# Decays, B and C of an SSD branch in scratch tables: another layout, another engine for the stores, an earlier place for sums and loads

## The chip, the cores and the metric

The kernel runs on one core of one Trainium2 chip, in one launch. The metric is device time in microseconds. Three runs of the kernel before took 1981.85, 1986.65 and 1986.39 us; their median is 1986.39 us. The profile is of one execution of its own.

## The reference

The reference is one inference step of a hybrid decoder layer in fp32, for a prompt of 256 tokens and, with the same weights, for 8 sample rows of one token each. With all widths written out:

```
h = RMSNorm(x)                                        # x: 256 + 8 rows of 2048
q, k, v, z, xbc, dt, qm, g = split(h @ w_in)          # w_in: 2048 x 13856
A = sliding-window attention(q, k, v)                 # 16 heads of 64, window 128
B = SSD(xbc, z, dt)                                   # 32 heads of 64 in 4 groups, state 128
M = attention of qm into 256 memory tokens            # 4 heads of 256
x = x + (sig(g0)*(A @ w_up_swa) + sig(g1)*(B @ w_up_ssd) + sig(g2)*(M @ w_up_mem)) @ w_out
x = x + (silu(h2 @ w_gate) * (h2 @ w_up)) @ w_down    # h2 = RMSNorm(x), width 5632
```

The part that the change touches is B, the SSD branch (a Mamba-2 scan in chunks). For the prompt there are two chunks of 128 tokens:

```
xbc = silu(causal conv of 4 taps(xbc));  x, B, C = split(xbc)      # B, C: 4 groups of 128
dt  = softplus(dt + dt_bias);  a = -exp(a_log)
acs = cumsum(dt * a) within the chunk                              # per token and head
decay[l, s] = exp(acs[l] - acs[s]) for s <= l, else 0
y   = sum over s of (C_l . B_s) * decay[l, s] * dt_s * x_s  +  (what the chunk before left) * exp(acs[l])  +  d_skip * x
```

For each of the 8 sample rows the scan is one step: the state (32 heads x 64 x 128) is multiplied by `exp(dt * a)`, `dt * x * B` is added, the new state is an output, and `y = state . C + d_skip * x`. Then y is multiplied by silu(z) and normed by group. The updated states, caches and conv buffers are outputs too.

## The kernel before

**Main stream.** All large products run on TensorE as a list of *units*. A unit is a weight tile of 512 KB (`raw`, 128 x 1024 fp32), loaded by SyncE (L230), split by ScalarE into a rounded part `hi` (L167) and by VectorE into the rest `lo` (L168), and used in 24 matmuls: eight pieces of the tile, each as hi x h_hi, hi x h_lo and lo x h_hi, so that the product keeps fp32 accuracy. Tokens are the moving side, 264 columns (256 prompt and 8 sample rows). `feed(i)` runs ahead of unit `i`: `N_DMA = 4` units in load, `N_SPLIT = 3` in the split, with four buffers for `raw` and three each for `hi` and `lo`.

**Order of the units.** Memory keys and values; then the groups of w_in for the memory queries, window queries, keys and values, the memory gates, B, C, dt; then, for the SSD groups g = 0 to 3, x and z (`x_group`, `z_group`), with the gates and the up-projection of the attention branch between them; the memory up-projection (`pum`); the SSD gates; the SSD up-projection (`pus`); the output projection; and, in three blocks, the feed-forward layers. In the profile's names `pin` is any group of w_in, `pua` the attention's up-projection.

**Side work.** Everything else is written as generators that yield an estimate of their time in us. After each unit the list `side` gets a credit of 1.0 and the list `slow` one of 0.75, at most 3.0 in hand, and the first task of each list runs while credit is left. In `side` stand, per SSD group, the conv (`V`, `ssd_conv_work`), the chunks (`X`, `ssd_chunk_work`) and the norm (`N`); ahead of them `task_b`, `task_c` and `task_dt`. In `slow` stand the memory attention of the sample rows and then, per group, their one-step scan (`Y`, `ssd_sample_work`), which may start when the group's chunks are written. Before the first unit of `pus` both lists are drained.

**The planner.** The kernel is traced in this order, but then a planner orders the instructions of each engine by a simulated time line (`schedule_with_timeline_sim=True`), hands out the tiles' buffers and places the semaphores. An engine takes its instructions in that order, and a DMA is issued by the engine that it is written for: when its wait is not over, all behind it on that engine waits too. Place in the source is thus a priority, not a time: in the profile the load of `bb` for group 0, written behind that group's chunks, goes out at 498 us, before them.

**Around the change.** `task_dt` turns dt to tokens x heads, takes the softplus (L1033 to L1045), and makes `da = dt * a` (L1062). Then come the sample rows' step sizes and factors (`dsc`, L1067 to L1083). Then the sums: `acs` by a matmul with a triangle of ones, once as tokens x heads (`acs_tok`) and once as heads x tokens, which ScalarE copies to `acsT` (L1093) and GpSimd stores to the DRAM scratch `acs_d` (L1094); with `wf` the weights of the chunk states are made. `task_c` puts B and C of the sample rows into the DRAM scratch `bc_d` (L1027). Both tables are there to be read back with one row broadcast to all 128 partitions:

- in `ssd_chunk_work`, per group and chunk, `dec` (L1156): 8 heads x 128 tokens of `acs_d`, 512 KB in SBUF. ScalarE turns it into the decay (L1165, L1166) and, for the second chunk, into `ce` (L1160); VectorE multiplies it by C . B (L1168); TensorE uses it (`py`);
- in `ssd_sample_work`, per group, `bb` and `cbs` (L1217, L1218): B and C of the 8 sample rows, 512 KB each. For each pair of heads there is a state tile `ld` (512 KB, loaded at L559 and stored at L1230); ScalarE scales it (L1225), VectorE adds `dx * bb` (L1226) and sums against `cbs` (L1227).

`dec`, `ce`, the conv's `acc` and `xs`, `y`, and the merge's `mgi` share four buffers (tag `t4`); `bb` and `cbs` share two (tag `lm`) with the tiles of the memory cache; `ld` has two of its own.

Before, `acs_d` is laid out as heads x 256 tokens, so that a `dec` load reads, for each partition, 8 runs of 512 bytes at a distance of 1 KB. `bc_d` is laid out as sample row x (B or C) x group x 128, so that `bb` reads 8 runs of 512 bytes at a distance of 4 KB.

Of the kernel before, what the change touches and what calls it, by code (L numbers as in the profile page):

```python
# [72 lines left out]
def tile_hybrid_decoder_step(  # L73
# [58 lines left out]
    def tiny(name, n):  # L132
        assert n <= 64
        return tp.tile([P, 64], F32, tag="tiny", name=nm(name), bufs=9)[:, 0:n]
# [826 lines left out]
    last = const([P, 11, 24], "last")  # L961
    acs_tok = const([P, 64], "acs_tok")
    wf = const([P, 96], "wf")
    acs_d = dr.tile([32, 256], F32, name="acs_d")
    bc_d = dr.tile([NS, 2, 4, P], F32, name="bc_d")

    def conv(ct, raw, dst):

# [47 lines left out]
    def task_c():  # L1016
        ssd["C"] = const([P, 4, NT], "CT")
        yield from conv(20, ssd["Craw"], ssd["C"])
        both = tiny("bcs", 64)
        for i, s in enumerate("BC"):  # L1020
            V.tensor_copy(both[:, 32 * i:32 * i + 32].rearrange("p (g b) -> p g b", g=4), ssd[s][:, :, NP:NT])
        ps = sps("bcr")
        tr(ps[0:64, 0:P], both)
        rows = t1("bcrows")[0:64, 0:P]
        act(rows, ps[0:64, 0:P], AF.Copy)
        for i in range(2):
            nc.gpsimd.dma_start(bc_d[:, i].rearrange("b g n -> g b n"), rows[32 * i:32 * i + 32])  # L1027
        yield 0.2

    def softplus(x, n, rows):  # L1030
# [17 lines left out]
    def task_dt():  # L1048
        ssd["dsc"] = const([P, 16, 17], "dsc", tag="nd")
        s3 = const([P, 3, 16, NS], "s3", tag="kT")  # L1050
        ssd["xsS"], ssd["zsS"], ssd["ysS"] = (s3[:, i] for i in range(3))
        raw = ssd["dtraw"]
        x = tiny("dtx", 64)
        ps = sps("dtT")
        for t in range(2):
            tr(ps[:, t * 32:(t + 1) * 32], raw[:, t * P:(t + 1) * P])
        V.tensor_tensor(x.rearrange("p (t h) -> p t h", t=2), ps[:, 0:64].rearrange("p (t h) -> p t h", t=2),
                        dtb_bc.unsqueeze(1).broadcast_to([P, 2, 32]), op=ALU.add)
        u, s = softplus(x, 64, P)
        V.scalar_tensor_tensor(dt_tok, u, 2.0, s, op0=ALU.mult, op1=ALU.add)  # L1060
        da = tiny("da", 64)
        V.tensor_tensor(da.rearrange("p (t h) -> p t h", t=2), dt_tok.rearrange("p (t h) -> p t h", t=2),  # L1062
                        na_bc.unsqueeze(1).broadcast_to([P, 2, 32]), op=ALU.mult)
        yield 3

        xs = tiny("dts", NS)[0:32]
        V.tensor_scalar(xs, raw[:, NP:NT], hcol[:, 0:1], None, op0=ALU.add)  # L1067
        u, s = softplus(xs, NS, 32)
        V.scalar_tensor_tensor(xs, u, 2.0, s, op0=ALU.mult, op1=ALU.add)
        dd = tiny("dds", NS)[0:32]  # L1070
        act(dd, xs, AF.Exp, scale=hcol[:, 1:2])
        ex = t2("ex")[0:32, 0:272].rearrange("p (j e) -> p j e", e=17)
        for o, src in ((0, xs), (8, dd)):
            V.tensor_tensor(ex[:, :, o:o + 8], src.unsqueeze(1).broadcast_to([32, 16, NS]),
                            jm.unsqueeze(2).broadcast_to([32, 16, NS]), op=ALU.mult)
        V.tensor_scalar(ex[:, :, 16], jm, hcol[:, 2:3], None, op0=ALU.mult)
        pr = tiny("pr", 2)
        V.tensor_reduce(pr[0:32], ident[0:32, 0:32].rearrange("h (j two) -> h two j", two=2), axis=AX.X, op=ALU.add)
        par = t1("par")[0:32, 0:P]
        V.tensor_copy(par.rearrange("h (two p) -> h two p", two=2), pr[0:32].unsqueeze(2).broadcast_to([32, 2, 64]))  # L1080
        ps = sps("dsc")
        mm(ps[:, 0:272], par, ex.rearrange("p j e -> p (j e)"))
        V.tensor_copy(ssd["dsc"].rearrange("p j e -> p (j e)"), ps[:, 0:272])  # L1083
        yield 3

        ps = sps("acs")
        mm(ps[:, 0:64], tri, da)
        mm(ps[:, 64:128], ones, da)
        for t in range(2):
            mm(ps[0:32, 128 + t * P:128 + (t + 1) * P], da[:, t * 32:(t + 1) * 32], tri)  # L1090
        V.tensor_copy(acs_tok, ps[:, 0:64])
        ac = t1("acsT")[0:32, 0:256]
        act(ac, ps[0:32, 128:384], AF.Copy)  # L1093
        nc.gpsimd.dma_start(acs_d, ac)  # L1094

        V.tensor_tensor(wf[:, 0:64], ps[:, 64:128], acs_tok, op=ALU.subtract)
        act(wf[:, 0:64], wf[:, 0:64], AF.Exp)
        act(wf[:, 64:96], ps[:, 96:128], AF.Exp)
        V.tensor_tensor(wf[:, 64:96], wf[:, 64:96], wf[:, 0:32], op=ALU.mult)
        yield 1  # L1100

    def ssd_conv_work(g):
        ssd[f"x{g}"] = t4("xs").rearrange("p (c n) -> p c n", c=4)
        yield from conv(4 * g, ssd[f"x{g}raw"], ssd[f"x{g}"])
# [1 line left out]
    def ssd_chunk_work(g):  # L1106
# [1 line left out]
        V.tensor_copy(ssd["xsS"][:, 4 * g:4 * g + 4], xs[:, :, NP:NT])  # L1108
        bT, cT, btok = ssd["B"], ssd["C"], ssd["Btok"]
        hs = slice(8 * g, 8 * g + 8)  # L1110
        xdt, xw = [], []

        def bc(v):
            return v.unsqueeze(2).broadcast_to([P, 8, 64])
# [1 line left out]
        def hp(v):  # L1116
            return v.rearrange("p (h d) -> p h d", d=64)

        for c in range(2):
            ps = sps("xtok")  # L1120
            for j in range(4):
                tr(ps[:, j * P:(j + 1) * P], xs[:, j, c * P:(c + 1) * P])
            d = t2("xdt")
            V.tensor_tensor(hp(d), hp(ps), bc(dt_tok[:, c * 32 + 8 * g:c * 32 + 8 * g + 8]), op=ALU.mult)
            xdt.append(d)
            yield 0.6
# [15 lines left out]
                            so.rearrange("p (j n) -> p j n", n=P))  # L1142
        yield 2
        y = t4("y").rearrange("p (c n) -> p c n", c=4)
        for c in range(2):
            cs = slice(c * P, (c + 1) * P)
            pc = sps("cb")
            mm(pc[:, 0:P], bT[:, g, cs], cT[:, g, cs])
            if c == 1:
                mm(pc[:, P:2 * P], bT[:, g, 0:P], cT[:, g, cs])  # L1150
            cb = t1("cb")[:, 0:(c + 1) * P]
            V.tensor_tensor(cb[:, 0:P], pc[:, 0:P], tri, op=ALU.mult)
            if c == 1:
                V.tensor_copy(cb[:, P:2 * P], pc[:, P:2 * P])
            a = t4("dec")[:, 0:1024].rearrange("p (h l) -> p h l", h=8)
            nc.gpsimd.dma_start(a, acs_d[hs, cs].unsqueeze(0).broadcast_to([P, 8, P]))  # L1156
            e = None
            if c == 1:
                e = t4("ce")[:, 0:1024].rearrange("p (h l) -> p h l", h=8)
                act(e, a, AF.Exp)  # L1160
                V.tensor_tensor(e, e, cb[:, P:2 * P].unsqueeze(1).broadcast_to([P, 8, P]), op=ALU.mult)
            yield 0.8
            for h in range(8):
                o = c * 32 + 8 * g + h
                act(a[:, h], a[:, h], AF.Relu, scale=-1.0, bias=acs_tok[:, o:o + 1])  # L1165
            act(a, a, AF.Exp, scale=-1.0)  # L1166
            yield 0.8
            V.tensor_tensor(a, a, cb[:, 0:P].unsqueeze(1).broadcast_to([P, 8, P]), op=ALU.mult)  # L1168
            yield 1.1
            py = sps("py")  # L1170
            for h2 in range(0, 8, 2):
                for m, (l, r) in enumerate(((xdt[c], a), (w, e))[:c + 1]):
                    for h in (h2, h2 + 1):
                        mm(py[(h % 2) * 64:(h % 2) * 64 + 64, (h // 2) * P:(h // 2 + 1) * P],
                           l[:, h * 64:(h + 1) * 64], r[:, h], start=m == 0, stop=m == c)
            for j in range(4):
                V.scalar_tensor_tensor(y[:, j, cs], xs[:, j, cs], ssd["dsc"][:, 4 * g + j, 16:17], py[:, j * P:(j + 1) * P],
                                       op0=ALU.mult, op1=ALU.add)
            yield 0.9
# [32 lines left out]
        yield 1.1  # L1212

    def ssd_sample_work(g):
        bb = lm("bb").rearrange("p (b n) -> p b n", b=NS)
        cb = lm("cbs").rearrange("p (b n) -> p b n", b=NS)
        nc.gpsimd.dma_start(bb, bc_d[:, 0, g].unsqueeze(0).broadcast_to([P, NS, P]))  # L1217
        nc.gpsimd.dma_start(cb, bc_d[:, 1, g].unsqueeze(0).broadcast_to([P, NS, P]))  # L1218
        for j in range(4 * g, 4 * g + 4):
            h = next(other_loads).rearrange("p (b n) -> p b n", b=NS)  # L1220
            dx = tiny("dx", NS)
            V.tensor_tensor(dx, ssd["xsS"][:, j], ssd["dsc"][:, j, 0:8], op=ALU.mult)
            jk = t1("jkh")[:, 0:P]
            for b in range(NS):
                act(h[:, b], h[:, b], AF.Copy, scale=ssd["dsc"][:, j, 8 + b:9 + b])  # L1225
                V.scalar_tensor_tensor(h[:, b], bb[:, b], dx[:, b:b + 1], h[:, b], op0=ALU.mult, op1=ALU.add)  # L1226
                V.tensor_tensor_reduce(jk, h[:, b], cb[:, b], 1.0, 0.0, ALU.mult, ALU.add, ssd["ysS"][:, j, b:b + 1])  # L1227
                if b % 4 == 3:
                    yield 2.0
            nc.gpsimd.dma_start(s_ssm[0, :, 2 * j:2 * j + 2].rearrange("b h p n -> (h p) b n"), h)  # L1230
# [386 lines left out]
```

## Time and profile before

| | |
|---|---|
| median of three runs | 1986.39 us (1981.85 to 1986.65) |
| the profiled execution, its own time | 1981.87 us |
| its span, first to last instruction | 1980.1 us |
| mean granted TensorE clock | 0.994 |
| matmuls on TensorE | 15436 |
| DMA, mean over the span | 202 GB/s, 400.78 MB |

The page gives for each engine the time in which it is busy. Matmuls are pipelined and their ends are modelled, so a busy PE need not be at its peak. "Idle before" and "released by" are inferred from semaphores. A DMA's time to landing runs from its issue to the last byte. q0 is the queue of DMAs that GpSimd issues in software, q1 that of the hardware queues. In rows of stretches the DMA share is the mean busy share of the core's 16 DMA engines.

### The profile page before, as it was taken

How to read it: one execution, taken by the hardware profiler on the slowest of the kernel's cores; microseconds unless marked ns; L12 is line 12 of the kernel's file. 1: busy time of each engine (PE TensorE's matmuls, PEld its weight loads, DVE VectorE, ACT ScalarE, POOL GpSimd, SP SyncE). 2: the span in 40 equal slices, each digit the busy share in tenths (PEclk: the TensorE clock that was granted, in tenths of full speed). 3: DMA queues.
4: the chain of work that ended last, by engine and by line, in shares of the span. 5: the costliest groups of instructions: out<-in, count | busy, mean ns of one | idle time of the engine just before them, and what ended most of it. 6: DMA issues, size and time to landing. Idle time of an engine off the chain costs nothing.

```text
span 1980.1 us, 37652 instructions
## 1 busy us (share of the span) xinstructions
PE 1937.3 (98%) x15436; PEld 1871.3 (95%) x15436; DVE 1159.3 (59%) x2217; ACT 970.8 (49%) x1419; POOL 122.6 (6%) x241
## 2 busy tenths in 40 slices
PE   8999999999898989999999999999999999999999
PEld 6799998889898989899999999999999999999998
DVE  6645577656486858568455556555545555445553
ACT  6544446656665575655444444444334444334443
POOL 3000110010101202111000000000000000000000
PEclk9999999999999999999999999999999999999999
DMA  8576677677678878779666556665556665566653
GB/s 283 192 221 206 204 210 232 199 220 232 172 203 223 249 195 252 243 268 334 186 192 191 183 164 178 181 181 180 181 181 174 184 185 180 182 179 180 181 188 130
DMA packets 190974, 400.78 MB, mean 202 GB/s; under 512 B 13491, under 2 KB 15714, under 8 KB 190664
## 3 DMA queue, kind: packets, MB, share of 16 engines
q1 hardware_dynamic: 169856, 324.13, 53.4%
q0 software_dynamic: 20944, 74.23, 12.6%
q8 instruction: 121, 1.98, 0.4%
q14 instruction: 53, 0.43, 0.1%
HBM read 376.53 MB, written 24.06 MB: 202 GB/s over the span
## 4 chain that ended last, share of the span: by engine, by line
PE 84%; DMA 7%; DVE 3%; issue 3%; ACT 1%; POOL 0%; SPq 0%; ACTq 0%; POOLq 0%
PE pin L146 22%; PE pu L146 13%; PE pdn L146 13%; PE pg L146 13%; PE pout L146 5%; PE pus L146 5%; PE pmem L146 5%; DMA raw<-in_w_in_dram 3%; PE pum L146 2%; DMA ld<-in_state_ssm_dram 1%; DVE lo L168 1%; PE pua L146 1%; DVE ld L1226 1%; DMA acs_d<-acsT 1%; PE po L146 1%
## 5 line engine op out<-in xcount | busy, mean ns | idle before, releaser
L168 DVE TENSOR_TENSOR lo<-raw,hi 128x1024 fp32r<-128x1024 f32 (+1 forms) x626 | 746.7, 1195 | 650.7 <-ACT hi L167 649.7
L167 ACT ACTIVATE hi<-raw 128x1024 fp32r<-128x1024 f32 (+1 forms) x626 | 646.0, 1036 | 869.4 <-PE pin L146 190.3
L146 PE MATMUL pin<-hh,hi 128*128 128x264 f32 x1728 | 494.7, 289 | 15.8 <-ACT hi L167 15.6
L146 PE MATMUL pin<-hl,hi 128*128 128x264 f32 x1728 | 493.3, 288 | 0.0
L146 PE MATMUL pin<-hh,lo 128*128 128x264 f32 x1728 | 483.7, 288 | 5.5 <-DVE lo L168 5.2
L146 PEld LDWEIGHTS pin<-hh,hi 128*128 128x128 f32 x1728 | 328.4, 190 | 22.9 <-ACT hi L167 18.2
L146 PEld LDWEIGHTS pin<-hh,lo 128*128 128x128 f32 x1728 | 322.2, 190 | 10.1 <-DVE lo L168 8.3
L146 PEld LDWEIGHTS pin<-hl,hi 128*128 128x128 f32 x1728 | 328.3, 190 | 3.3 <-issue 2.5
L146 PE MATMUL pdn<-fah,hi 128*128 128x264 f32 x704 | 199.7, 285 | 0.0
L146 PE MATMUL pdn<-fal,hi 128*128 128x264 f32 x704 | 199.4, 285 | 0.0
L146 PE MATMUL pu<-h2h,hi 128*128 128x264 f32 x704 | 199.4, 284 | 0.0
L146 PE MATMUL pu<-h2l,hi 128*128 128x264 f32 x704 | 199.3, 284 | 0.0
L146 PE MATMUL pg<-h2l,hi 128*128 128x264 f32 x704 | 199.1, 285 | 0.0
L146 PE MATMUL pg<-h2h,hi 128*128 128x264 f32 x704 | 198.4, 284 | 0.0
L146 PE MATMUL pdn<-fah,lo 128*128 128x264 f32 x704 | 197.0, 284 | 0.0
L146 PE MATMUL pu<-h2h,lo 128*128 128x264 f32 x704 | 196.6, 284 | 0.0
L146 PE MATMUL pg<-h2h,lo 128*128 128x264 f32 x704 | 196.1, 284 | 0.0
L146 PEld LDWEIGHTS pdn<-fah,hi 128*128 128x128 f32 x704 | 132.7, 189 | 0.1
L146 PEld LDWEIGHTS pu<-h2h,hi 128*128 128x128 f32 x704 | 132.7, 189 | 0.0
L146 PEld LDWEIGHTS pg<-h2h,hi 128*128 128x128 f32 x704 | 132.7, 188 | 0.0
L146 PEld LDWEIGHTS pdn<-fal,hi 128*128 128x128 f32 x704 | 132.6, 188 | 0.1
L146 PEld LDWEIGHTS pu<-h2l,hi 128*128 128x128 f32 x704 | 132.6, 188 | 0.0
(511 smaller groups left out, 2964.7 us busy)
## 6 DMA issues: line engine op xcount, KB each, us to landing
raw<-in_w_in_dram SPq DMA_DIRECT2D x218, 512.0 KB, 4.5
raw<-in_w_gate_dram SPq DMA_DIRECT2D x88, 512.0 KB, 3.7
raw<-in_w_up_dram SPq DMA_DIRECT2D x88, 512.0 KB, 3.9
raw<-in_w_down_dram SPq DMA_DIRECT2D x88, 512.0 KB, 4.0
raw<-in_w_mem_kv_dram SPq DMA_DIRECT2D x32, 512.0 KB, 5.2
raw<-in_w_up_ssd_dram SPq DMA_DIRECT2D x32, 512.0 KB, 3.8
raw<-in_w_out_dram SPq DMA_DIRECT2D x32, 512.0 KB, 3.7
ld<-in_cache_mem_k_dram POOLq DMA_DIRECT2D x16, 512.0 KB, 5.5
```

The costliest lines, as they stand in the source:

```text
L146: nc.tensor.matmul(out, lhsT=lhsT, rhs=rhs, start=start, stop=stop)
L167: act(hi, src, AF.Copy)
L168: V.tensor_tensor(lo, src, hi.bitcast(F32), op=ALU.subtract)
L1226: V.scalar_tensor_tensor(h[:, b], bb[:, b], dx[:, b:b + 1], h[:, b], op0=ALU.mult, op1=ALU.add)
```

## The change

- The scratch `acs_d` becomes group x chunk x head of the group x token, and `bc_d` becomes (B or C) x group x sample row x 128. A table that one load reads is then 4 KB in one piece, and a helper `to_all` broadcasts it to the 128 partitions, on GpSimd's queue as before.
- The stores into both tables are issued by ScalarE instead of GpSimd: one for `bc_d` instead of two, two for `acs_d` (one per chunk) instead of one.
- In `task_dt` the sums stand right behind `da`, ahead of the sample rows' step sizes.
- In `ssd_chunk_work` the two `dec` tiles of a group are loaded ahead: the first at the head of the group's work, the second ahead of the loop over the chunks.
- In `ssd_sample_work` a `yield 3.0` stands between the loads of `bb` and `cbs` and the first state tile.

```diff
--- before.py
+++ after.py
@@ -961,8 +961,12 @@
     last = const([P, 11, 24], "last")
     acs_tok = const([P, 64], "acs_tok")
     wf = const([P, 96], "wf")
-    acs_d = dr.tile([32, 256], F32, name="acs_d")
-    bc_d = dr.tile([NS, 2, 4, P], F32, name="bc_d")
+
+    acs_d = dr.tile([4, 2, 8, P], F32, name="acs_d")
+    bc_d = dr.tile([2, 4, NS, P], F32, name="bc_d")
+
+    def to_all(dst, row):
+        nc.gpsimd.dma_start(dst, row.rearrange("a n -> (a n)").unsqueeze(0).broadcast_to([P, 1024]))
 
     def conv(ct, raw, dst):
 
@@ -1023,8 +1027,7 @@
         tr(ps[0:64, 0:P], both)
         rows = t1("bcrows")[0:64, 0:P]
         act(rows, ps[0:64, 0:P], AF.Copy)
-        for i in range(2):
-            nc.gpsimd.dma_start(bc_d[:, i].rearrange("b g n -> g b n"), rows[32 * i:32 * i + 32])
+        nc.scalar.dma_start(bc_d.rearrange("i g b n -> (i g b) n"), rows)
         yield 0.2
 
     def softplus(x, n, rows):
@@ -1062,6 +1065,23 @@
         V.tensor_tensor(da.rearrange("p (t h) -> p t h", t=2), dt_tok.rearrange("p (t h) -> p t h", t=2),
                         na_bc.unsqueeze(1).broadcast_to([P, 2, 32]), op=ALU.mult)
         yield 3
+
+        ps = sps("acs")
+        mm(ps[:, 0:64], tri, da)
+        mm(ps[:, 64:128], ones, da)
+        for t in range(2):
+            mm(ps[0:32, 128 + t * P:128 + (t + 1) * P], da[:, t * 32:(t + 1) * 32], tri)
+        V.tensor_copy(acs_tok, ps[:, 0:64])
+        ac = t1("acsT")[0:32, 0:256]
+        act(ac, ps[0:32, 128:384], AF.Copy)
+        for c in range(2):
+            nc.scalar.dma_start(acs_d[:, c], ac[:, c * P:(c + 1) * P])
+
+        V.tensor_tensor(wf[:, 0:64], ps[:, 64:128], acs_tok, op=ALU.subtract)
+        act(wf[:, 0:64], wf[:, 0:64], AF.Exp)
+        act(wf[:, 64:96], ps[:, 96:128], AF.Exp)
+        V.tensor_tensor(wf[:, 64:96], wf[:, 64:96], wf[:, 0:32], op=ALU.mult)
+        yield 1
 
         xs = tiny("dts", NS)[0:32]
         V.tensor_scalar(xs, raw[:, NP:NT], hcol[:, 0:1], None, op0=ALU.add)
@@ -1083,22 +1103,6 @@
         V.tensor_copy(ssd["dsc"].rearrange("p j e -> p (j e)"), ps[:, 0:272])
         yield 3
 
-        ps = sps("acs")
-        mm(ps[:, 0:64], tri, da)
-        mm(ps[:, 64:128], ones, da)
-        for t in range(2):
-            mm(ps[0:32, 128 + t * P:128 + (t + 1) * P], da[:, t * 32:(t + 1) * 32], tri)
-        V.tensor_copy(acs_tok, ps[:, 0:64])
-        ac = t1("acsT")[0:32, 0:256]
-        act(ac, ps[0:32, 128:384], AF.Copy)
-        nc.gpsimd.dma_start(acs_d, ac)
-
-        V.tensor_tensor(wf[:, 0:64], ps[:, 64:128], acs_tok, op=ALU.subtract)
-        act(wf[:, 0:64], wf[:, 0:64], AF.Exp)
-        act(wf[:, 64:96], ps[:, 96:128], AF.Exp)
-        V.tensor_tensor(wf[:, 64:96], wf[:, 64:96], wf[:, 0:32], op=ALU.mult)
-        yield 1
-
     def ssd_conv_work(g):
         ssd[f"x{g}"] = t4("xs").rearrange("p (c n) -> p c n", c=4)
         yield from conv(4 * g, ssd[f"x{g}raw"], ssd[f"x{g}"])
@@ -1108,7 +1112,11 @@
         V.tensor_copy(ssd["xsS"][:, 4 * g:4 * g + 4], xs[:, :, NP:NT])
         bT, cT, btok = ssd["B"], ssd["C"], ssd["Btok"]
         hs = slice(8 * g, 8 * g + 8)
-        xdt, xw = [], []
+        xdt, dec = [], []
+
+        def load_dec(c):
+            dec.append(t4("dec")[:, 0:1024])
+            to_all(dec[c], acs_d[g, c])
 
         def bc(v):
             return v.unsqueeze(2).broadcast_to([P, 8, 64])
@@ -1116,6 +1124,7 @@
         def hp(v):
             return v.rearrange("p (h d) -> p h d", d=64)
 
+        load_dec(0)
         for c in range(2):
             ps = sps("xtok")
             for j in range(4):
@@ -1142,6 +1151,7 @@
                             so.rearrange("p (j n) -> p j n", n=P))
         yield 2
         y = t4("y").rearrange("p (c n) -> p c n", c=4)
+        load_dec(1)
         for c in range(2):
             cs = slice(c * P, (c + 1) * P)
             pc = sps("cb")
@@ -1152,8 +1162,7 @@
             V.tensor_tensor(cb[:, 0:P], pc[:, 0:P], tri, op=ALU.mult)
             if c == 1:
                 V.tensor_copy(cb[:, P:2 * P], pc[:, P:2 * P])
-            a = t4("dec")[:, 0:1024].rearrange("p (h l) -> p h l", h=8)
-            nc.gpsimd.dma_start(a, acs_d[hs, cs].unsqueeze(0).broadcast_to([P, 8, P]))
+            a = dec[c].rearrange("p (h l) -> p h l", h=8)
             e = None
             if c == 1:
                 e = t4("ce")[:, 0:1024].rearrange("p (h l) -> p h l", h=8)
@@ -1212,10 +1221,11 @@
         yield 1.1
 
     def ssd_sample_work(g):
-        bb = lm("bb").rearrange("p (b n) -> p b n", b=NS)
-        cb = lm("cbs").rearrange("p (b n) -> p b n", b=NS)
-        nc.gpsimd.dma_start(bb, bc_d[:, 0, g].unsqueeze(0).broadcast_to([P, NS, P]))
-        nc.gpsimd.dma_start(cb, bc_d[:, 1, g].unsqueeze(0).broadcast_to([P, NS, P]))
+        bb, cb = lm("bb"), lm("cbs")
+        to_all(bb, bc_d[0, g])
+        to_all(cb, bc_d[1, g])
+        bb, cb = (t.rearrange("p (b n) -> p b n", b=NS) for t in (bb, cb))
+        yield 3.0
         for j in range(4 * g, 4 * g + 4):
             h = next(other_loads).rearrange("p (b n) -> p b n", b=NS)
             dx = tiny("dx", NS)
```

## The prediction

> **What bounds the kernel now.** First the page: its span, the engines' shares, the slices and the chain that ended last.
>
> ```profile
> span 1980.1 us, 37652 instructions
> PE 1937.3 (98%) x15436; PEld 1871.3 (95%) x15436; DVE 1159.3 (59%) x2217; ACT 970.8 (49%) x1419; POOL 122.6 (6%) x241
> ...
> PE 84%; DMA 7%; DVE 3%; issue 3%; ACT 1%; POOL 0%; SPq 0%; ACTq 0%; POOLq 0%
> ```
>
> TensorE sets the end, but the chain leaves it for 7% of the span, through DMA. Second, the chain in order of time says where (start, length, link):
>
> ```profile
> 501.84 12.25 DMA acs_d<-acsT
> 514.37 4.86 DMA dec<-acs_d
> 522.68 1.24 DVE lo L168
> ...
> 613.41 20.63 DMA raw<-in_w_in_dram
> ...
> 681.42 18.36 DMA raw<-in_w_in_dram
> ...
> 784.43 20.03 DMA raw<-in_w_in_dram
> ...
> 1001.28 94.10 PE pus L146 x768
> ```
>
> There is one place per SSD group: at 502 us the store and reload of the decays, and at 613, 681 and 784 us a weight tile (`raw`) that takes about 20 us to land. Third, the table of engine time by stretch. Columns: stretch, length, busy us of PE, PEld, DVE, ACT and POOL (with instructions), granted clock, DMA share, GB/s.
>
> ```profile
> 460.00:490.00 30.00, 30.00 (x253) 28.72 (x250) 22.33 (x59) 16.17 (x25) 2.95 (x5) 1.00 0.72 227
> ...
> 500.00:530.00 30.00, 23.28 (x179) 22.78 (x178) 12.01 (x17) 16.90 (x30) 3.18 (x4) 0.89 0.69 170
> 610.00:650.00 40.00, 33.08 (x294) 31.41 (x293) 21.79 (x53) 23.33 (x38) 4.00 (x5) 0.96 0.82 206
> 680.00:720.00 40.00, 32.76 (x252) 31.78 (x252) 22.70 (x51) 26.31 (x50) 4.40 (x5) 0.91 0.84 216
> 780.00:820.00 40.00, 35.62 (x261) 34.23 (x260) 19.43 (x36) 21.01 (x35) 5.09 (x7) 0.91 0.94 267
> 890.00:930.00 40.00, 38.76 (x313) 38.07 (x312) 38.48 (x130) 18.81 (x33) 8.17 (x11) 1.00 1.00 364
> 940.00:1000.00 60.00, 60.00 (x496) 60.00 (x495) 28.39 (x41) 27.96 (x37) 0.00 (x0) 1.00 0.64 188
> ```
>
> From 500 to 820 us, in four stretches, PE is idle 6.72 + 6.92 + 7.24 + 4.38 = 25.3 us. The clock granted there is under 1.00, which costs at most busy time x what is missing: 23.28 x 0.11 + 33.08 x 0.04 + 32.76 x 0.09 + 35.62 x 0.09 = 10.0 us. So these stalls cost 25.3 to 35.3 us: 9.3 at the first, then 8.2, 10.2 and 7.6. This is all that the change can reach; from 940 us on PE has no gap.
>
> What makes `raw` late? DMA is as busy there as at 890 to 930 us, but moves little: 206 to 267 GB/s against 364. The issues show the odd ones beside a load of the same size (KB each, median us to landing):
>
> ```profile
> qb<-qd POOLq DMA_DIRECT2D x8, 512.0 KB, 6.4
> bb<-bc_d POOLq DMA_DIRECT2D x4, 512.0 KB, 13.0
> cbs<-bc_d POOLq DMA_DIRECT2D x4, 512.0 KB, 14.7
> ```
>
> And GpSimd's order of issue puts them at every stall (`cbs` right behind, or some us later):
>
> ```profile
> 498.08 0.92 POOL L1217 DMA_DIRECT2D bb<-bc_d  x1 [23.43 <-PE oms L146]
> ...
> 607.13 0.88 POOL L1217 DMA_DIRECT2D bb<-bc_d  x1
> ...
> 677.91 0.89 POOL L1217 DMA_DIRECT2D bb<-bc_d  x1
> ...
> 779.55 0.89 POOL L1217 DMA_DIRECT2D bb<-bc_d  x1
> ```
>
> **Part 1: `bc_d` laid out as it is read.** Each of the eight loads of B and C now reads, for every partition, eight runs of 512 bytes that lie 4 KB apart; changed, it reads one run of 4 KB, which is exactly the form of `qb<-qd`. Price of the two forms, from the DMA view of three stretches, where software-issued packets (q0) are almost only those: 500 to 512 us (`bb`, `cbs`), 279 to 288 us (two `qb` and one cache tile), 515 to 521 us (two `dec`). Columns: packets, MB, share of 16 engines.
>
> ```profile
> q0 software_dynamic: 345, 1.11, 63.6%
> raw<-in_w_in_dram SPq DMA_DIRECT2D x3, 512.0 KB, 10.4
> ```
> ```profile
> q0 software_dynamic: 428, 1.57, 57.4%
> raw<-in_w_in_dram SPq DMA_DIRECT2D x2, 512.0 KB, 4.3
> ```
> ```profile
> q0 software_dynamic: 288, 1.05, 55.3%
> ```
>
> All DMA engines together spend 0.636 x 12 / 1.11 = 6.9 us per MB on `bb`/`cbs`, 0.574 x 9 / 1.57 = 3.3 on `qb`, 0.553 x 6 / 1.05 = 3.2 on `dec`. So the 1.05 MB of one group cost 7.2 us of DMA time and should cost 3.5: 3.7 us less per group. The whole stretches say more. Priced like 890 to 930 us (share 1.00 for 364 GB/s), 610 to 650 us should have needed 206 / 364 = 0.57 of the time instead of 0.82, which is 10.2 us too much; likewise 9.9 and 8.3 us at 680 and 780. Priced like the plain weight stream at 940 to 1000 us (0.64 for 188 GB/s), the excess is only 4.8, 4.2 and 1.3 us. Bounds per group are thus 1.3 and 10.2 us; I take 6, midway between the 3.7 measured on the loads themselves and the 8 to 10 of the stretches with a like mix.
>
> DMA time becomes PE time through the lateness of `raw`. In the views of 607 to 616, 678 to 686 and 779 to 800 us the weight tiles have these landings; the fourth row is 890 to 930 us:
>
> ```profile
> raw<-in_w_in_dram SPq DMA_DIRECT2D x4, 512.0 KB, 16.1
> raw<-in_w_in_dram SPq DMA_DIRECT2D x4, 512.0 KB, 18.4
> raw<-in_w_in_dram SPq DMA_DIRECT2D x5, 512.0 KB, 18.7
> raw<-in_w_in_dram SPq DMA_DIRECT2D x12, 512.0 KB, 9.2
> ```
>
> A tile is asked for four units ahead (`N_DMA`). A unit is 24 matmuls of 60.00 / 496 us, 2.9 us, so the lead is 11.6 us, of which the split into lo (1.24 us in the chain) and hi (1.04, below) takes 2.3. Slack: 9.3 us. Today's overshoot is 6.8 + 9.1 + 9.4 = 25.3 us, close to the 26.0 us lost in those stretches, and at 9.2 us of landing only 1.24 us in 40 are idle: the model holds. With 6 us less the overshoot is 0.8 + 3.1 + 3.4 = 7 us, so 19 of 26 us come back. At 3.7 us less per group 11 come back; at 8.8 (the mean of the first three excesses and the 6.7 us of 500 to 530) nearly all, 25; with the low prices 4.8 + 4.2 + 1.3 = 10.
>
> A rule of the Trainium skill speaks against this part: "DMA: Bandwidth & Descriptors", Specifications, gives 512 B as the least transfer for line rate, so runs of 512 B would already be at it, and by that the part is worth nothing. The trace agrees for `dec` (also runs of 512 B) and not for `bb`.
>
> **Part 2: decays first, stored by ScalarE, loaded at the head of a group.** When is what ready, and who waits? Timeline of VectorE, then of ScalarE:
>
> ```profile
> 475.58 0.23 DVE L1062 TENSOR_TENSOR da<-dt_tok,na_bc 128x64 f32<-128x64 f32 x1
> ```
> ```profile
> 496.15 4.80 ACT L1225 ACTIVATE ld<-ld,dsc 128x128 f32<-128x128 f32 x16 [0.70 <-DVE dsc L1083]
> 500.86 0.36 ACT L1093 ACTIVATE acsT<-acs 32x256 f32<-32x256 f32 x1
> ...
> 519.25 2.44 ACT L1165 ACTIVATE dec<-dec,acs_tok 128x128 f32<-128x128 f32 x8 [9.22 <-DMA dec<-acs_d]
> 521.60 1.04 ACT L167 ACTIVATE hi<-raw 128x1024 fp32r<-128x1024 f32 x1
> ```
>
> `da`, all that the sums need, is there at 475.8 us; the sums were written behind the sample group's step sizes and reached ScalarE at 500.9, behind sixteen state copies. The store then sat behind `bb` and `cbs` in GpSimd's queue. Ahead of these, it can be issued near 480 us, land in some 5 us, and `dec` 5 us later (4.86 above), by 490: ScalarE wants it at 510. Queued behind ScalarE's wait of 9.22 us is the split (521.60) for which PE stands still, so the wait is worth the whole first stall, 9.3 us; a landing of 10.4 us for `raw` in that stretch would leave 1.1 us of it with the old layout, and nothing with the new. I take 8.8; bounds 4 (the loads are not really earlier, but the queue ahead of the store is shorter by 3.7) and 9.3.
>
> What it adds: three DMA issues on ScalarE. At GpSimd's 0.92 us each that is 2.8 us at most, and at least nothing; ScalarE has 13.8 us idle at 460 to 490 us to cover them. GpSimd loses three issues; nothing waits for it there. The four sums, moved ahead, are the same matmuls. `dec` of a group's second half now takes one of the four `t4` buffers before the first half is computed; in group 0 both loads already went out in one go, and what comes late for it is a partial sum of the merge (`mgi`), needed only after its eight weight tiles: nothing.
>
> **Part 3: `yield 3.0` in the sample groups** puts their work four units (11.7 us) later, each group. The last group's lies in the stretch of 890 to 930 us (VectorE 38.5 of 40 us busy), so it would end near 942, and its results are needed at 1001, where the SSD up-projection (`pus`) starts. Cost nothing: VectorE has 31.6 us idle at 940 to 1000.
>
> **Sum.** 19 + 8.8 = 27.8 us; less 1 for the bounds above: 27 us against the profiled execution of 1981.87 us (span 1980.1), 1955. The shown median, 1986.39, is 4.5 us higher, the runs falling at 1981.9 and 1986.5; I add half of that: **1957 us**.
>
> **Rivals.**
> A, transfers bunched anyway (chance 0.14). State tiles, merge tiles and weights still meet at the same places, and only the low price of a lone weight stream is saved: 10 + 8.8 = 19 us, 1965 with the same half. For it: at 890 to 930 DMA is full without these loads. Against it: PE hardly stalls there.
> B, the layout is inert (0.06): slow because 128 partitions read the same few lines, which stays. Then only the first stall goes, 8: 1976. Against it: `qb` reads that way and is fast. The rule named above would lead here.
> C, slower (0.06): a new wait. The consumers move up with the loads, and ScalarE, whose queue holds the splits, stands at `dec` in every half. Three waits for `dec` are in the view of waits:
>
> ```profile
> ACT dec L1165 <- DMA dec<-acs_d: 10.0, 2, 9.2
> ACT ce L1160 <- DMA dec<-acs_d: 7.0, 1, 7.0
> ```
>
> 17.0 / 3 = 5.7 us each; at all eight halves 45 us, less 27 gained: 18 us slower, 2002. It decides from a mean of 27 / 8 = 3.4 us per half. Against it: five of eight loads are waited for by none, and the yields between load and use (0.6 + 0.6 + 2) are three units, 9 us.
> D, the change doesn't do what it says (0.10): the planner already issues loads when a buffer is free, whatever their place (`bb` went out at 498 us, long before group 0's results). Then the first stall shrinks only by 4: 19 + 4 = 23 us, 1961.
> My forecast: 0.60. The last 0.04 is no change, from a planner's order that gives all of it back.
>
> **Numbers.** A measurement of this kernel can tell 0.3%, 6 us, from no change. Forecast, A, D and 0.04 of B lie beyond it: faster 0.88. Same: the rest of B and 0.04, 0.06. Slower: C, 0.06. The range goes from the whole 35.3 us with nothing given back and the low run level, 1946, to B, 1976; C, part of B, no change, and a gain beyond the stalls are left out.
>
> **What would show it.** Part 1: `bb` and `cbs` land in 6 to 8 us, and no `raw` over 13 us between 480 and 830. Part 2: ScalarE's wait of 9.22 us is gone, `acs_d` is stored before 490 us, and 500 to 530 has under 1 us of PE idle. Part 3: no wait at the start of the up-projection. Wrong if `bb` still needs 13 us (B), if `raw` is late though `bb` is quick (A), if ScalarE waits for `dec` in several halves (C), or if idle time turns up elsewhere before 1001 us.

## The result, and the profile after

The changed kernel takes 1951.16 us (median of four runs, 1949.37 to 1952.73); beside it on the same chip the kernel before takes 1985.49 us. The ratio is 0.9834, with a 95% interval of 0.9822 to 0.9846: 34 us, or 1.7%, faster. The forecast was 1957 us and 27 us of gain. The two profiled executions are 1981.87 and 1951.31 us, 30.6 us apart.

First the page of the changed kernel: span, the engines' shares, and the chain that ended last.

```profile
span 1949.6 us, 37668 instructions
...
PE 1927.4 (99%) x15436; PEld 1863.8 (96%) x15436; DVE 1160.9 (60%) x2217; ACT 972.0 (50%) x1420; POOL 115.2 (6%) x238
...
PE 89%; DMA 4%; issue 3%; DVE 2%; ACT 1%; POOL 0%; SPq 0%; ACTq 0%; POOLq 0%; DVEq 0%
```

The span less PE's busy time is PE's idle time: 1980.1 - 1937.3 = 42.8 us before, 1949.6 - 1927.4 = 22.2 us now, so 20.6 us less. The same 15436 matmuls are busy for 9.9 us less; this is the clock, whose mean rose from 0.994 to 0.999. Together 30.5 us, all of the difference. DMA has gone from 7% to 4% of the chain.

Then the table by stretch (columns as in the prediction). The stalls used to lie at 500, 613, 681 and 784 us; what follows the first now comes some 6 to 22 us sooner.

```profile
500.00:530.00 30.00, 30.00 (x256) 29.68 (x255) 17.65 (x23) 20.73 (x34) 0.88 (x1) 1.00 0.67 205
...
600.00:650.00 50.00, 47.79 (x426) 46.36 (x425) 42.77 (x130) 31.22 (x52) 7.99 (x11) 1.00 0.81 246
650.00:720.00 70.00, 67.70 (x575) 66.42 (x574) 48.66 (x106) 51.29 (x92) 7.74 (x11) 1.00 0.80 249
720.00:780.00 60.00, 60.00 (x520) 59.72 (x519) 48.96 (x148) 37.58 (x63) 11.03 (x15) 1.00 0.93 291
780.00:820.00 40.00, 40.00 (x333) 40.00 (x332) 26.25 (x36) 27.00 (x42) 4.16 (x7) 1.00 0.79 254
```

PE loses 0 + 2.2 + 2.3 + 0 + 0 = 4.5 us here, where it lost 25.3 in four narrower stretches before (25.9 in these same five), and the clock is 1.00 throughout. The DMA engines are about as busy as they were, but move 246 to 291 GB/s in the four later rows, where it was 206 to 267 at the three later stalls.

The issues of the changed kernel (KB each, median us from issue to landing), and then the software queue from 497 to 506 us, where `bb` and `cbs` of the first group are nearly alone in it (packets, MB, share of 16 engines):

```profile
dec<-acs_d POOLq DMA_DIRECT2D x8, 512.0 KB, 7.1
bb<-bc_d POOLq DMA_DIRECT2D x4, 512.0 KB, 7.8
cbs<-bc_d POOLq DMA_DIRECT2D x4, 512.0 KB, 7.0
```
```profile
q0 software_dynamic: 320, 1.08, 33.8%
```

`bb` lands in 7.8 instead of 13.0 us, `cbs` in 7.0 instead of 14.7. Their price is 0.338 x 9 / 1.08 = 2.8 us of DMA time per MB, where it was 6.9. The weight tiles of the three later stretches (598 to 625, 664 to 690, 757 to 785 us) follow:

```profile
raw<-in_w_in_dram SPq DMA_DIRECT2D x4, 512.0 KB, 6.3
```
```profile
raw<-in_w_in_dram SPq DMA_DIRECT2D x8, 512.0 KB, 4.7
```
```profile
raw<-in_w_in_dram SPq DMA_DIRECT2D x9, 512.0 KB, 11.9
```

Before they took 16.1, 18.4 and 18.7 us. These are medians of the few tiles whose landing the trace holds, and the windows are longer now; the latest tile of each stretch is a fairer measure: 6.3, 10.0 and 11.9 us now, 20.6, 21.4 and 20.0 before. The last row has a lesson: from 757 to 785 us tiles still land in 11.9 us, and PE loses nothing there (60.00 of 60.00, 40.00 of 40.00). Last, ScalarE and GpSimd near the first stall:

```profile
481.13 0.36 ACT L1076 ACTIVATE acsT<-acs 32x256 f32<-32x256 f32 x1
481.58 1.16 ACTq L1078 DMA_DIRECT2D acs_d<-acsT  x1
482.77 0.60 ACTq L1078 DMA_DIRECT2D acs_d<-acsT  x1
...
496.11 2.43 ACT L1174 ACTIVATE dec<-dec,acs_tok 128x128 f32<-128x128 f32 x8
```
```profile
484.08 0.53 POOL L969 DMA_DIRECT2D dec<-acs_d  x1 [8.85 <-ACT wf L1082]
485.18 0.53 POOL L969 DMA_DIRECT2D dec<-acs_d  x1 [0.57 <-DMA acs_d<-acsT]
497.43 0.53 POOL L969 DMA_DIRECT2D bb<-bc_d  x1 [11.72 <-PE oms L146]
```

The sums come 20 us sooner (481.13, before 500.86), the two stores go out at 481.58 and 482.77 us and have landed when the second `dec` goes out at 485.18, and ScalarE uses `dec` at 496.11 with no wait. The group of waits "ACT dec" is gone from the view of waits.

### The profile page after: what moved, and what is told of

It is laid out like the page before. It is cut to its first block, busy times and chain, and to the rows that moved or that the text cites. A ratio compares the mean times of both kernels' runs of the same rounds, so it can differ in the third digit from the quotient of the medians.

```text
span 1949.6 us, 37668 instructions
## 1 busy us (share of the span) xinstructions
PE 1927.4 (99%) x15436; PEld 1863.8 (96%) x15436; DVE 1160.9 (60%) x2217; ACT 972.0 (50%) x1420; POOL 115.2 (6%) x238
## 4 chain that ended last, share of the span: by engine, by line
PE 89%; DMA 4%; issue 3%; DVE 2%; ACT 1%; POOL 0%; SPq 0%; ACTq 0%; POOLq 0%; DVEq 0%
PE pin L146 26%; PE pu L146 13%; PE pdn L146 13%; PE pg L146 13%; PE pout L146 5%; PE pus L146 5%; PE pmem L146 5%; PE pua L146 2%; PE pum L146 1%; DMA ld<-in_state_ssm_dram 1%; PE po L146 1%; PE py L146 1%; PE ps L146 1%; DMA ld<-in_cache_mem_v_dram 1%; DMA ld<-in_cache_mem_k_dram 1%
```

## The experiments

Each was timed beside the kernel before. Ratios are to that, with 95% intervals; between chips the kernel before moves by some us, so ratios are what to compare.

**1. The layout of B and C alone.** The kernel before, with only the new `bc_d` and its broadcast; GpSimd still stores.

```diff
-    bc_d = dr.tile([NS, 2, 4, P], F32, name="bc_d")
+    bc_d = dr.tile([2, 4, NS, P], F32, name="bc_d")
...
-        for i in range(2):
-            nc.gpsimd.dma_start(bc_d[:, i].rearrange("b g n -> g b n"), rows[32 * i:32 * i + 32])
+        nc.gpsimd.dma_start(bc_d.rearrange("i g b n -> (i g b) n"), rows)
...
-        nc.gpsimd.dma_start(bb, bc_d[:, 0, g].unsqueeze(0).broadcast_to([P, NS, P]))
-        nc.gpsimd.dma_start(cb, bc_d[:, 1, g].unsqueeze(0).broadcast_to([P, NS, P]))
+        to_all(bb, bc_d[0, g])
+        to_all(cb, bc_d[1, g])
```

> The kernel before, with only the scratch of B and C laid out as it is read (one store by GpSimd instead of two; the decays as before, no yield). Theory (the loads of B and C hold up the weight tiles): 20 to 26 us faster than before, so 1960 to 1966 us; bb and cbs land in 6 to 9 us instead of 13 to 15; the first stall shrinks, since the store of the decays sits behind shorter loads, but ScalarE still waits some 4 to 6 us there. Rival (the layout is inert, the gain comes from the earlier place of sums and loads): within 3 us of before, about 1985, and bb and cbs still land in 13 us.

Measured: 1953.19 us, ratio 0.9847 (0.9831 to 0.9864), 28 us under the 1981.34 of the kernel before and 2 more than the expectation's upper end. `bb` and `cbs` land in 7.4 and 7.2 us, as expected. Its stretches:

```profile
500.00:530.00 30.00, 26.82 (x209) 26.42 (x208) 14.19 (x18) 18.10 (x31) 3.23 (x4) 0.94 0.65 194
600.00:650.00 50.00, 48.51 (x442) 47.03 (x442) 40.70 (x115) 33.15 (x58) 8.36 (x11) 1.00 0.86 261
650.00:720.00 70.00, 69.09 (x588) 68.07 (x588) 53.02 (x124) 52.04 (x93) 8.08 (x10) 1.00 0.82 252
780.00:820.00 40.00, 39.82 (x329) 39.61 (x328) 26.60 (x36) 27.59 (x43) 3.64 (x6) 1.00 0.77 248
```

The three later stalls are gone (1.5, 0.9 and 0.2 us idle, clock 1.00), and the first is halved: 3.2 us idle plus 26.82 x 0.06 = 1.6 us of clock, where it was 9.3. The layout does nearly all of the work, and reaches into the first stall: the store of the decays, issued behind `bb` and `cbs`, took 12.2 us to land in the kernel before and takes 4.0 here.

**2. The decays alone.** The changed kernel with the old `bc_d`, its stores back on GpSimd, and no yield in the sample groups.

```diff
-    bc_d = dr.tile([2, 4, NS, P], F32, name="bc_d")
+    bc_d = dr.tile([NS, 2, 4, P], F32, name="bc_d")
...
-        nc.scalar.dma_start(bc_d.rearrange("i g b n -> (i g b) n"), rows)
+        for i in range(2):
+            nc.gpsimd.dma_start(bc_d[:, i].rearrange("b g n -> g b n"), rows[32 * i:32 * i + 32])
...
-        to_all(bb, bc_d[0, g])
-        to_all(cb, bc_d[1, g])
-        yield 3.0
+        nc.gpsimd.dma_start(bb, bc_d[:, 0, g].unsqueeze(0).broadcast_to([P, NS, P]))
+        nc.gpsimd.dma_start(cb, bc_d[:, 1, g].unsqueeze(0).broadcast_to([P, NS, P]))
```

> The changed kernel with the old scratch of B and C (512-byte runs 4 KB apart, stored by GpSimd) and without the yield: the work on the decays alone. Theory: 6 to 9 us faster than before, 1977 to 1980 us; the wait of ScalarE for dec in the first group is gone, weight tiles still land 14 to 20 us after their issue in the later groups. Rival: most of the gain, 25 to 33 us, so 1953 to 1960 us.

Measured: 1977.26 us, ratio 0.9976 (0.9964 to 0.9988): 4 us gained, under the 6 to 9 expected. Two of its stretches, then its chain, then ScalarE:

```profile
500.00:530.00 30.00, 30.00 (x256) 29.68 (x256) 17.67 (x24) 20.85 (x35) 1.28 (x2) 1.00 0.81 205
600.00:650.00 50.00, 41.41 (x353) 40.44 (x352) 31.42 (x94) 24.77 (x46) 6.66 (x8) 0.90 0.85 213
```
```profile
601.05 11.01 DMA ld<-in_state_ssm_dram
```
```profile
612.17 2.45 ACT L1235 ACTIVATE ld<-ld,dsc 128x128 f32<-128x128 f32 x8 [6.86 <-DMA ld<-in_state_ssm_dram]
614.52 2.93 ACT L167 ACTIVATE hi<-raw 128x1024 fp32r<-128x1024 f32 x3
626.69 2.44 ACT L1235 ACTIVATE ld<-ld,dsc 128x128 f32<-128x128 f32 x8 [9.23 <-issue]
```

The first stall is fully gone, 9.3 us. But the next stretch loses 8.6 us idle and 41.41 x 0.10 = 4.1 of clock, 12.7 us. The kernel before lost 6.9 + 43.08 x 0.03 = 8.2 there:

```profile
600.00:650.00 50.00, 43.08 (x382) 41.09 (x381) 30.19 (x79) 29.94 (x55) 7.53 (x9) 0.97 0.82 217
```

With slow `bb` and `cbs` ahead of it in GpSimd's queue, a state tile issued at 601.05 lands after 11.0 us and one issued at 608.45 after 18.2. ScalarE, with splits behind it, stands 6.86 and then 9.23 us in front of the two (the second is put down to "issue"; the tile landed at 626.62, and ScalarE went on at 626.69). So about half of the gain is given back a hundred us on. The expectation had not foreseen this second way of being late.

**3. The change without the yield.** Only `yield 3.0` is left out.

```diff
-        yield 3.0
```

> The changed kernel without the yield of 3.0 in the sample groups. Theory: the yield is worth nothing, within 3 us of the changed kernel's 1951 us. Rival (the yield spreads the sample groups' transfers and with them the weight tiles' lateness): 5 to 15 us slower than the changed kernel, 1956 to 1966 us.

Measured: 1948.88 us, ratio 0.9827 (0.9812 to 0.9841), which the changed kernel's 0.9834 can't be told from. Against experiments 1 and 2, in the same session, it prices the parts: the layout on top of the decays 1977.26 - 1948.88 = 28.4 us, the decays on top of the layout 1953.19 - 1948.88 = 4.3 us.

**4. The runs stay short, their distance changes.** The changed kernel, but `bb` and `cbs` read eight runs of 512 bytes again, at a distance of 4.5 KB instead of 4 KB: the table is as before, with a row of padding.

```diff
-    bc_d = dr.tile([2, 4, NS, P], F32, name="bc_d")
+    bc_d = dr.tile([NS, 9, P], F32, name="bc_d")
...
-        to_all(bb, bc_d[0, g])
-        to_all(cb, bc_d[1, g])
+        nc.gpsimd.dma_start(bb, bc_d[:, g].unsqueeze(0).broadcast_to([P, NS, P]))
+        nc.gpsimd.dma_start(cb, bc_d[:, 4 + g].unsqueeze(0).broadcast_to([P, NS, P]))
```

> The changed kernel, with B and C still read in eight runs of 512 bytes, but 4.5 KB apart instead of 4 KB (the scratch has a ninth, unused row of 512 bytes per sample row). If the distance of exactly 4 KB made the loads slow: as the changed kernel, 1949 to 1954 us, bb and cbs land in 7 to 9 us. If short runs that lie far apart made them slow: as with the old table, 1967 to 1977 us, bb and cbs land in 12 to 15 us.

Measured: 1955.23 us, ratio 0.9861 (0.9843 to 0.9880). The software queue from 500 to 511 us:

```profile
q0 software_dynamic: 320, 1.08, 30.6%
```

0.306 x 11 / 1.08 = 3.1 us per MB, and `bb` and `cbs` land in 8.4 us each. The first alternative held, with a time 1 us beyond its range. Eight short runs are nearly as cheap as one long one; 512 bytes more of distance give back most of what the layout gives. The layout of the change also shortens GpSimd's issue of `bb`, from a median of 0.89 us to 0.56; here it is 0.89 as before, so that is not what made the loads slow.

**5. Less lead.** `N_DMA` and the buffers of `raw` go from four to three, in the kernel before and in the changed one, so that a tile is asked for one unit (2.9 us) later.

```diff
-    N_DMA, N_SPLIT = 4, 3
+    N_DMA, N_SPLIT = 3, 3
...
-            raw = wp.tile([P, 1024], F32, tag="raw", name=nm("raw"), bufs=4)
+            raw = wp.tile([P, 1024], F32, tag="raw", name=nm("raw"), bufs=3)
```

In the kernel before:

> The kernel before with three raw buffers and N_DMA = 3: every weight tile is asked for one unit (2.9 us) later. Theory (TensorE stands still by as much as the latest weight tile exceeds the lead): each of the four stalls grows by one unit, 9 to 12 us slower than before. Rival (ScalarE is held by the late state tiles in its queue, and the weight tiles are late without effect): within 3 us of before.

In the changed kernel:

> The changed kernel with three raw buffers and N_DMA = 3. Its latest weight tiles land after 6.3, 10.0 and 11.9 us at the places of the former stalls and nothing stalls there. Theory: with a lead of 8.7 us the last two stall by some 1 and 3 us, and the stretch at 860 to 900 us by as much, 4 to 8 us slower than the changed kernel's 1951 us. Rival: within 3 us of it.

Measured: 2008.77 us, ratio 1.0135 (1.0112 to 1.0157), and 1978.87 us, ratio 0.9985 (0.9974 to 0.9995). The kernel before loses 27 us, the changed one 28 in time and 30 by the ratios; none of the expectations holds. Two stretches of the changed kernel with three buffers:

```profile
720.00:780.00 60.00, 54.73 (x486) 53.51 (x484) 43.14 (x144) 29.56 (x46) 9.38 (x12) 0.99 0.85 244
...
880.00:940.00 60.00, 52.70 (x404) 52.04 (x404) 47.73 (x158) 27.19 (x45) 8.16 (x11) 0.94 0.88 295
```

From 720 to 780 us, where tiles landed late without harm at four units, PE now loses 5.3 us, and from 880 to 940 us 7.3. By the span less the busy time, the changed kernel has 1977.3 - 1937.1 = 40.2 us of idle PE instead of 22.2, and 9.7 us more busy time for the same matmuls; the kernel before goes from 42.8 to 2006.9 - 1947.2 = 59.7 us idle and 9.9 us more busy. So the direction holds: lateness beyond the lead is what costs. The size doesn't follow from a slack minus a landing at four places; about two thirds are stalls, spread over more places, and the rest is clock that goes with them.

**6. One group out of four with the slow table.** The changed kernel, in which `bb` and `cbs` of group 1 alone read from a second table in the old layout.

```diff
+    bo_d = dr.tile([NS, 2, 4, P], F32, name="bo_d")
...
+        if g == 1:
+            for i, t in enumerate((bb, cb)):
+                nc.gpsimd.dma_start(t.rearrange("p (b n) -> p b n", b=NS),
+                                    bo_d[:, i, g].unsqueeze(0).broadcast_to([P, NS, P]))
```

> The changed kernel, with the slow table (512-byte runs 4 KB apart, a second scratch) for B and C of group 1 alone; the other three groups read the new table. Theory: the stall at group 1 comes back alone, 6 to 9 us slower than the changed kernel, 1957 to 1960 us, with TensorE idle 5 us or more between 600 and 650 us and none at groups 0, 2 and 3. Rival (the gain is the planner's order, not the table): less than 3 us slower, or stalls at places other than group 1.

Measured: 1954.96 us, ratio 0.9866 (0.9847 to 0.9886). That is 4 us more than the changed kernel in time and 0.32%, 6 us, in ratio, so at or under the low end of what was expected. Its stretch of that group:

```profile
600.00:650.00 50.00, 45.41 (x393) 43.99 (x393) 39.10 (x120) 28.68 (x49) 6.12 (x8) 0.97 0.83 230
```

4.6 us idle and 45.41 x 0.03 = 1.4 of clock, against 2.2 us: 3.8 us, at this place and no other (67.80 of 70 us, 60.00 of 60 and 40.00 of 40 in the stretches up to 820). Here `bb` and `cbs` landed in 9.4 and 9.2 us, and the state tile behind them in 11.2. A single slow group costs less than its quarter of the 28 us. The same slow loads of this group took 12.8 and 16.9 us in the kernel before, where GpSimd issued them 7.4 us apart with a `dec` load between; here they go out 18.4 us apart, with no `dec` between. So landings seem to get longer when such loads meet, but no run separates this.

**7. and 8. Distances of 2 and 8 KB.** As experiment 4, but with the runs 2 KB apart (tables for B and C each by themselves) and 8 KB apart (16 rows per sample row).

```diff
-    bc_d = dr.tile([2, 4, NS, P], F32, name="bc_d")
+    bc_d = dr.tile([2, NS, 4, P], F32, name="bc_d")
...
-    bc_d = dr.tile([2, 4, NS, P], F32, name="bc_d")
+    bc_d = dr.tile([NS, 16, P], F32, name="bc_d")
```

At 2 KB:

> The changed kernel, but bb and cbs read 8 runs of 512 B that lie 2 KB apart. Theory (the distance decides, and the price doubles with it from some distance on: 1 KB 3.2 us of DMA time per MB in the dec loads, 4 KB 6.9, 8 KB 12.0): 2 KB is at 3.2 to 4.0 us per MB, bb and cbs land in 7 to 9 us, and the time is that of the changed kernel, 1950 to 1955 us. Rival (every distance of a power of two that makes the runs return to the same place is slow, only dec's 1 KB is let off): about 5 us per MB, bb and cbs over 10 us, 1957 to 1966 us.

At 8 KB:

> The changed kernel with B and C read in runs of 512 bytes that lie 8 KB apart. If distances that are a multiple of 4 KB are slow: bb and cbs land in 12 to 17 us and the time is 1967 to 1980 us. If 4 KB alone was special: 7 to 9 us, and 1950 to 1957 us.

Measured: at 2 KB 1959.02 us, ratio 0.9889 (0.9873 to 0.9905); at 8 KB 2002.47 us, ratio 1.0101 (1.0079 to 1.0124), slower than the kernel before. The software queue at the first pair of loads, from 497 to 512 us at 2 KB and from 499 to 524 us at 8 KB:

```profile
q0 software_dynamic: 320, 1.08, 35.1%
```
```profile
q0 software_dynamic: 320, 1.08, 51.9%
```

0.351 x 15 / 1.08 = 4.9 and 0.519 x 25 / 1.08 = 12.0 us per MB. At 2 KB the theory fell; its rival had the price and the time right, and the landings of `bb` and `cbs`, 9.9 us each, just under its 10. At 8 KB the first alternative held and was too mild: `bb` and `cbs` land in 15.9 and 21.3 us. The price and the time go together:

| what `bb` and `cbs` read for a partition | DMA time per MB | ratio |
|---|---|---|
| one run of 4 KB (the change) | 2.8 us | 0.9834 |
| 8 runs of 512 B, 4.5 KB apart | 3.1 us | 0.9861 |
| 8 runs, 2 KB apart | 4.9 us | 0.9889 |
| 8 runs, 4 KB apart (experiment 2) | 6.9 us (kernel before; 7.1 in experiment 2, 497 to 512 us) | 0.9976 |
| 8 runs, 8 KB apart | 12.0 us | 1.0101 |

In the first three rows each ratio's interval overlaps the next one's, so neighbours there are told apart by price alone; the rows of 4 and 8 KB are clear of all others. Experiment 2 also lacks the yield, which experiment 3 found to be worth nothing. From the first row to the last, 9.2 us per MB over four groups of 1.05 MB are 39 us of DMA time, and the kernel loses 0.0267 of about 1982 us, 53 us. Up to 4 KB it is 17 us of DMA time for 28 us of kernel. At 8 KB ScalarE's waits from 440 to 1000 us show both ways of being late:

```profile
ACT hi L167 <- DMA raw<-in_w_in_dram: 48.6, 10, 11.1
ACT ld L1236 <- DMA ld<-in_state_ssm_dram: 32.2, 8, 10.7
```

**9. The sums first, nothing else of the decays' part.** Experiment 1 with the sums and their store moved ahead of the sample rows' step sizes. GpSimd stores, `acs_d` has its old layout, `dec` is loaded at its old place.

```diff
+        ps = sps("acs")
+        mm(ps[:, 0:64], tri, da)
...
+        nc.gpsimd.dma_start(acs_d, ac)
...
+        yield 1
+
         xs = tiny("dts", NS)[0:32]
...
-        ps = sps("acs")
-        mm(ps[:, 0:64], tri, da)
...
-        nc.gpsimd.dma_start(acs_d, ac)
```

> The kernel before with the layout of bc_d and with the sums and their store moved ahead of the sample rows' step sizes; GpSimd still issues the stores, and dec is loaded where it was. Theory (the place of the sums is what ends the first stall): acs_d is stored before 490 us, 500 to 530 us has under 1 us of PE idle, and the time is 1948 to 1953 us. Rival (the store has to leave GpSimd's queue, or the loads have to move): 500 to 530 keeps about the 3.2 us that the layout alone leaves, and the time is that of the layout alone, 1952 to 1956 us.

Measured: 1948.55 us, ratio 0.9834 (0.9819 to 0.9848). The first stretch:

```profile
500.00:530.00 30.00, 30.00 (x256) 29.68 (x256) 17.01 (x21) 18.74 (x33) 1.76 (x2) 1.00 0.75 226
```

The theory held: `acs_d` is stored at 482.4 us, the stall is gone, and the time can't be told from the changed kernel's. The new layout of `acs_d`, ScalarE's stores and the earlier place of the loads aren't needed for it.

**10. ScalarE's stores, nothing else of the decays' part.** Experiment 1 with both stores on ScalarE; the sums stay late.

```diff
-        nc.gpsimd.dma_start(bc_d.rearrange("i g b n -> (i g b) n"), rows)
+        nc.scalar.dma_start(bc_d.rearrange("i g b n -> (i g b) n"), rows)
...
-        nc.gpsimd.dma_start(acs_d, ac)
+        nc.scalar.dma_start(acs_d, ac)
```

> The kernel before with the layout of bc_d and with the stores into both tables on ScalarE; the sums stay where they were. Theory (the sums are late, not the store's queue): acsT is still made near 500 us, dec is issued near 506, ScalarE still waits 4 to 6 us for it, 500 to 530 us keeps 2 to 3.2 us of PE idle, and the time is 1951 to 1956 us. Rival (the queue is what made the store late): 500 to 530 has under 1 us idle, and 1948 to 1951 us.

Measured: 1948.86 us, ratio 0.9834 (0.9818 to 0.9850). The first stretch, then ScalarE:

```profile
500.00:530.00 30.00, 29.86 (x252) 29.16 (x251) 16.50 (x22) 19.85 (x35) 2.66 (x3) 1.00 0.72 235
```
```profile
501.78 0.36 ACT L1095 ACTIVATE acsT<-acs 32x256 f32<-32x256 f32 x1
502.17 0.36 ACTq L1096 DMA_DIRECT2D acs_d<-acsT  x1
...
512.85 2.45 ACT L1167 ACTIVATE dec<-dec,acs_tok 128x128 f32<-128x128 f32 x8 [1.93 <-DMA dec<-acs_d]
```

The theory fell and its rival held: the sums are as late as ever (501.78), yet 0.1 us is left of the stall. The same places in experiment 1, GpSimd and then ScalarE:

```profile
503.38 0.88 POOL L716 DMA_DIRECT2D m_d<-omsT  x1 [5.21 <-issue]
504.17 0.61 POOL L1096 DMA_DIRECT2D acs_d<-acsT  x1
```
```profile
515.55 2.45 ACT L1167 ACTIVATE dec<-dec,acs_tok 128x128 f32<-128x128 f32 x8 [5.38 <-DMA dec<-acs_d]
```

There the store goes out 2 us later, behind a store of the memory branch, and ScalarE stands 5.38 us instead of 1.93. The 3.5 us are enough. With the fast layout either of two small moves ends the first stall; the second adds nothing. The stall's end is seen in the stretches; by the ratios alone, 0.9834 in both, these kernels can't be told from experiment 1's 0.9847 (0.9831 to 0.9864).

## Why the prediction was right, and where its steps were wrong

The total was right: 27 us forecast, 30.6 us between the profiled executions. Its two parts were sized wrongly in opposite directions, 9 us too little and nearly 5 too much, so that the total came this close is partly luck.

**What bounds the kernel.** Right. The four stretches held 25.3 us of idle and at most 10.0 us of clock; 20.6 us of idle and 9.9 us of busy time went. The clock term, called an upper bound, was in fact that large.

**Part 1, the layout: 19 us forecast, 28 us measured** (28.4 on top of the decays, 28 alone). The mechanism was right: `bb` and `cbs` land in 7.8 and 7.0 us, the tiles behind them in 4.7 to 11.9. The term that was mis-sized is "I take 6" us per group, midway, and with it the 7 us of overshoot that were to stay; the upper case, nearly all 25, was the true one. On the loads themselves 6.9 - 2.8 = 4.1 us per MB went, 4.3 us per group, near the 3.7 of the prediction; but the latest weight tiles of the three stretches came 14.3, 11.4 and 8.1 us sooner, where 6 were taken for each. Two things stood behind it. The slack of 9.3 us was too small, there at least: tiles that land in 11.9 us cost PE nothing at 757 to 785 us. And lateness was taken to pass through `raw` alone: experiment 2 shows the state tiles as a second way, and experiment 1 shows the layout taking 9.3 - 4.8 = 4.5 us off the first stall, which the sum had put almost wholly to part 2.

A rule of the Trainium skill stood against this part ("DMA: Bandwidth & Descriptors", Specifications: line rate from 512 B on). At 4.5 KB the trace agrees with it, 3.1 us per MB against 2.8 for whole runs. At 2, 4 and 8 KB it doesn't, with runs of the same 512 bytes: the rule has no word on distance, and distance is what decided. The prediction rejected the rule on the right rows (`bb` against `dec`, both with runs of 512 bytes), but it priced the old form as a whole and did not say that the distance sets the price.

**Part 2, the decays: 8.8 us forecast, some 4 us measured** (4.3 on top of the layout, 4 alone). The lower bound, 4, was the true value, for reasons that the bound did not name. With the layout only 4.8 us of the first stall were left to win. Without it all 9.3 us were won, and half was lost again at 600 to 650 us. That ScalarE wanted the decays at about 510 us, and that the wait blocked a split, was right. That all the pieces act together was wrong: experiments 9 and 10 show two that each suffice. The place of the loads isn't needed, though no run moved it alone: in experiment 9, with the loads at their old place in the source, the first `dec` still goes out at 486.9 us.

**Part 3, the yield: nothing, as forecast.** Experiment 3; in the changed kernel PE is idle for 1.5 of the 1006 us from 940 to 1946.

**The rivals.** A (transfers bunched anyway, 1965): fell; the transfers still meet, with a DMA share of 0.79 to 0.93, but they are short enough. B (the layout inert, 1976): fell for this layout; experiment 2 is the kernel B would have given, 1977. C (ScalarE stands at `dec`, 2002): fell; no such wait is left. D (the placement inert, 1961): half right. The loads' place adds nothing, as it said; the stall goes all the same, since with the fast layout the store's 2 us were enough.

**The lead model.** It was called a model that holds because its overshoot of 25.3 us met a loss of 26.0. Experiments 5 and 6 say that this agreement was partly luck: a unit of lead costs 27 to 30 us in either kernel, not the few us that four overshoots give, and one slow group alone costs 4 to 6 us.

**What stays open.** Why runs at 2, 4 and 8 KB are slow and those at 4.5 KB aren't was not tried further; the runs show the dependence, not its cause. Nor is it settled why a unit of lead costs both kernels about the same, though one of them has hardly a stall left.

## What to carry to other kernels

Price a broadcast read by its DMA time per MB in a stretch where it is nearly alone, and compare it with a plain read of the same size: here the gap cost the kernel more than the DMA time itself (28 us for 17), through what landed behind it in the queues. When two parts of a change attack the same wait, price each with the other already done, and ask which of its pieces alone is enough. If the layout of a scratch table can't be made contiguous, try one row of padding: 512 bytes on a distance of 4 KB gained most of it here. Distances of 2 and 8 KB were slow too, but were not tried with padding.

## What the runs showed of the hardware that was not expected

The DMA time of a read of 512-byte runs, broadcast to 128 partitions, depends on the distance of the runs: 3.1 us per MB at 4.5 KB, but 4.9 at 2 KB, 6.9 at 4 KB and 12.0 at 8 KB; the old `dec` loads, 1 KB apart, cost 3.2. The Trainium skill ("DMA: Bandwidth & Descriptors", Latency and other measured facts) tells of a like effect in copies between HBM tensors, for row pitches of 512 KiB and more at large powers of two, healed by a few KiB of padding. Here 512 bytes of padding at 4 KB were enough, at distances a hundred times smaller; whether it is the same cause, no run here shows.

The clock that the throttle granted followed the stalls: 0.89 to 0.96 in the prediction's four stretches with 4.4 to 7.2 us of idle PE each, 1.00 in the stretches that hold the same work now. It took 9.9 us of busy time beside 20.6 us of idle, so on the mean each us of stall that went brought half a us more. It isn't a steady rate: in finer stretches of the kernel before, the clock is 0.50 from 520 to 526, 626 to 628, 701 to 707 and 797 to 802 us, right in or behind the four stalls, and 1.00 between them. Nor does every stall bring such a stretch: with three buffers the kernel before loses 4.2 us from 880 to 940 us, at a clock of 1.00.
